# A float32 decoder layer on one core: weights and operands count as ready when their low parts are done, the output projection's late operands are split in its order, and the first two row tiles load first

## The chip, the cores and the metric

The kernel runs on one core of one Trainium2 chip. The time is that of one execution on the device, in microseconds (us); less is better. A core has engines that each run their own instructions in order: TensorE (PE in the rows: matmuls and transposes), VectorE (DVE), ScalarE (ACT), GpSimd (POOL) and SyncE (SP, which here only issues transfers). They wait for each other through semaphores.

## The reference

It is one decoder layer on 512 rows of 1024 float32 values: RMSNorm, an input projection, two token mixers (retention and a gated delta rule) merged by gates, an output projection with a residual, then a gated MLP with a causal convolution.

```python
def reference(x, ...):                      # x (1, 512, 1024) float32
    u = rmsnorm(x, g)
    ret_q, ret_k, ..., gates = split(u @ w_in)
    o_r = retention_chunkwise(...)          # 8 heads
    o_d = gated_delta_chunkwise(...)        # 8 heads, a triangular solve per 128 rows
    h = x + merged(o_r, o_d, gates) @ w_o   # the output projection
    return rmsnorm(h + conv_ffn(rmsnorm(h)))
```

## The kernel before

**Products in parts.** TensorE multiplies float32 values as sums of parts. `split` makes of an operand a high part (a cast, on ScalarE) and a low part (operand minus high part, on VectorE). `weights()` does the same for the weights, in 212 blocks of 128x1024 that are loaded to `wraw`, cast to `whi` and subtracted to `wlo`; four blocks are held at a time. A product is then three matmuls, a **triple**: weight high with operand high, weight high with operand low, weight low with operand high. `take()` gives the next block to a product and holds TensorE's order until the block is in `ready`.

**How the order is made.** The order of instructions on every engine is fixed when the program is built. A planner (`Order`) keeps a clock that TensorE's planned work moves on and for each engine a time at which it is free; tasks (Python generators, started with `spawn`) issue their instructions when the clock passes their time, and `yield 0.3` puts a task off by 0.3 planned us. `hold(cond)` runs tasks until `cond` is met, so that a matmul is placed behind the instructions that make its operands. These times only set the order; on the chip the engines wait for what they need.

**The stages.** The start loads the rows of x in four row tiles of 128 (two halves each), scales them (`norm_in`) and transposes them. The mixing phase follows (projections `pk`, `pq`, `pv`, `pr`, `pz`; two triangular solves in steps `pm`, for which a solved block goes through DRAM, `x_dram`, and comes back as `tt`). Then come four products of 1024x1024 (`py`, whose sums are `res`).

The **output projection** (`po`) is computed as seven products of quarter matrices, p = 0, 5, 2, 3, 4, 1, 6 in that order, with the operands B11, B22, T2, T1, T3, B21, T4. Each has two row tiles (t = 0, 1), four triples each, and two weight blocks; its blocks are #112 to #125. `m_out` takes the transposed merged rows (`mr`, a copy by ScalarE out of `pmt`), forms the operands' sums on VectorE (`mt`: T3 = B22 - B12, T2 = B11 - T3, T1 = B11 - B12, T4 = -T2 - B21) and starts `o_split` for each, whose high and low parts appear as `mB` and `mT`. `o_into` adds a finished product into `h` on VectorE; a row tile of `h` that is complete gets its sum of squares (`junk`, ScalarE), `rs` (VectorE), `rr` (a power, GpSimd), its scaling (`hs`), transposes (`pt`) and the split to `u2hi` (ScalarE) and `u2lo` (VectorE). Row tiles 2 and 3 are complete before 0 and 1; h_20 below is tile 2's first half.

The **FFN** (`pa`, `pb`) starts on row tiles 2 and 3 and takes in tiles 0 and 1 as they come; its weight blocks (`w_up`) begin with #126. The down projection (`pd`) follows.

The names above are those in the rows: an output, an arrow and the inputs. A helper records all of VectorE's and ScalarE's instructions, so that they all have line 200, and all matmuls have line 215, transposes 219.

Of the kernel before, what the change touches and what calls it, by code (L numbers as in the profile page):

```python
# [13 lines left out]
AF = mybir.ActivationFunctionType  # L14
ALU = mybir.AluOpType
# [40 lines left out]
HK = KT // 2  # L56
# [37 lines left out]
BLOCKS = weight_blocks()  # L94
# [3 lines left out]
class Order:  # L98
# [29 lines left out]
    def spawn(self, gen, after=0.0):  # L128
        self.n += 1
        heapq.heappush(self.tasks, ((self.clock if self.now is None else self.now) + after, self.n, gen))  # L130
# [91 lines left out]
def body(nc, tc, ctx, io):  # L222
    sp = nc.sync
    order = Order()
    spawn, poll, hold = order.spawn, order.poll, order.hold
    vec = Engine(order, "vec", nc.vector, vec_cost)
    act = Engine(order, "act", nc.scalar, act_cost)
# [15 lines left out]
    def S(name, dt=F32):  # L243
        return heap.tile([P, T], dt, name=name, tag="s", bufs=HEAP)
# [90 lines left out]
    def weights():  # L335
        i = count["split"]
        if i == len(BLOCKS):
            return
        count["split"] += 1
        while i not in raws:  # L340
            yield 0.3
        raw = raws.pop(i)
        n = raw.shape[1]
        hi = wp.tile([P, n], F32R, name="whi", tag="whi", bufs=WB)
        act.copy(hi, raw)
        yield

        n_ = 0
        while order.free.get("vec", 0.0) > order.now + 0.8 and n_ < 12:
            n_ += 1  # L350
            yield 0.3
        lo = wp.tile([P, n], F32R, name="wlo", tag="wlo", bufs=WB)
        vec.tensor_tensor(lo, raw, hi.bitcast(F32), ALU.subtract)
        ready[i] = (hi, lo)
        yield
        free[0] += 1
        fetch()

# [130 lines left out]
    full = slice(0, T)  # L489
# [34 lines left out]
    def split(dst_hi, dst_lo, src, scale=None):  # L524

        if scale is None:
            act.copy(dst_hi, src)
            yield
            vec.tensor_tensor(dst_lo, src, dst_hi.bitcast(F32), ALU.subtract)
        else:  # L530
            act.activation(dst_hi, src, AF.Identity, scale=scale)
            yield
            vec.scalar_tensor_tensor(dst_lo, src, scale, dst_hi.bitcast(F32), ALU.mult, ALU.subtract)

    def transpose4(src, name):
        pt = PS(name)
# [8 lines left out]
    for t in range(NT):  # L545
        for i in range(2):
            sp.dma_start(x_in[t][i], xv[t, :, ck(i, T)])
        if t == 0:
            sp.dma_start(cst, io["cst"][:, :256])
        if t == 1:  # L550
            sp.dma_start(prm, io["prm"])
            fetch()
    free[0] = 1
# [13 lines left out]
    def norm_in(t):  # L567
        xs = [S(f"xs{t}{i}") for i in range(2)]
        ssq = s4("ssqx", 2)
        for i in range(2):  # L570
            half_ssq(ssq, i, x_in[t][i], xs[i])
        yield
        rr = s4("rr", 1)
        yield from row_scale(ssq, rr)
        yield
        vec.tensor_scalar(xs[0], x_in[t][0], rr, None, ALU.mult)
        if t < 2:
            act.activation(xs[1], x_in[t][1], AF.Identity, scale=rr)
        else:
            pool.tensor_scalar(xs[1], x_in[t][1], rr, None, ALU.mult)  # L580
        xs_all[t] = xs

    for t in range(NT):
        spawn(norm_in(t), (3.4, 4.9, 11.0, 12.6)[t])

    def fetch_more():
        while "G" not in have:
# [665 lines left out]
    def o_get(name, k, t):  # L1253
        return (name, t) in o_opnd and tuple(a[:, ck(k)] for a in o_opnd[name, t])

    def o_split(name, t, src):
        hi, lo = S(f"m{name}", F32R), S(f"m{name}", F32R)
        yield from split(hi, lo, src)
        o_opnd[name, t] = hi, lo

    def m_out(t, i, r):
        yield 0.2
        pt = transpose4(r, "pmt")
        yield
        name, half = f"B{i + 1}{t // 2 + 1}", t % 2
        m = o_raw[name, half] = S(f"mr{t}{i}")
        act.copy(m, pt)
        yield
        if name in ("B11", "B21", "B22"):
            spawn(o_split(name, half, m))  # L1270
        if name == "B12":
            t3 = S("mt3")
            vec.tensor_tensor(t3, o_raw["B22", half], m, ALU.subtract)
            t2 = o_raw["T2", half] = S("mt2")
            vec.scalar_tensor_tensor(t2, t3, -1.0, o_raw["B11", half], ALU.mult, ALU.subtract)
            spawn(o_split("T2", half, t2), 0.2)
            yield 2.5
            t1 = S("mt1")
            vec.tensor_tensor(t1, o_raw["B11", half], m, ALU.subtract)
            spawn(o_split("T1", half, t1), 0.2)  # L1280
            yield 2.5
            spawn(o_split("T3", half, t3), 0.2)
        elif name == "B21":
            yield 1.5
            t4 = S("mt4")
            vec.scalar_tensor_tensor(t4, o_raw["T2", half], -1.0, m, ALU.mult, ALU.subtract)
            spawn(o_split("T4", half, t4), 0.2)
# [59 lines left out]
    h1 = [[None] * 2 for _ in range(NT)]  # L1347
# [13 lines left out]
    def o_into(t, i, ps, op, last=False):  # L1361

        vec.tensor_tensor(h1[t][i], h1[t][i], ps, op)
        yield
        if not last:
            return
        junk = S("junk")
        act.activation(junk, h1[t][i], AF.Square, scale=1.0 / 32.0, accum_out=ssqs[t][:, i:i + 1])
        if i == 0:
            return  # L1370
        yield
        rr = s4("rr", 1)
        yield from row_scale(ssqs[t], rr)
        yield
        for i2 in range(2):
            xs = S("hs")
            vec.tensor_scalar(xs, h1[t][i2], rr, None, ALU.mult)
            spawn(u2_out(t, i2, xs), 0.6 * (i2 + 1))

    u2_ready = set()  # L1380
# [12 lines left out]
    def fourth(t, ps):  # L1393
        yield from o_into(2 + t, 1, ps, ALU.subtract)
        yield from o_into(2 + t, 0, ps, ALU.add, True)

    def bank():
        return [PS("po") for _ in range(2)]

    A = bank()  # L1400
    product(0, o_get, HK, [[(full, A[t], True, o_into(t, 0, A[t], ALU.add))] for t in range(2)])
    E = bank()
    product(5, o_get, HK, [[(full, E[t], True, o_into(2 + t, 0, E[t], ALU.add))] for t in range(2)])
    product(2, o_get, HK, [[(full, A[t], False, o_into(2 + t, 0, A[t], ALU.add))] for t in range(2)])
    F = bank()
    product(3, o_get, HK, [[(full, F[t], True, fourth(t, F[t]))] for t in range(2)])
    product(4, o_get, HK, [[(full, A[t], False, o_into(2 + t, 1, A[t], ALU.subtract, True))] for t in range(2)])
    C = bank()
    product(1, o_get, HK, [[(full, C[t], True, o_into(t, 0, C[t], ALU.add, True))] for t in range(2)])
    product(6, o_get, HK, [[(full, A[t], False, o_into(t, 1, A[t], ALU.subtract, True))] for t in range(2)], tail=2)  # L1410
    u2 = (u2hi, u2lo)
    spawn(presums(presum((DOWN,), 4), (order.clock, order.clock + 200.0, 32)))

# [138 lines left out]
    F = [PS("pd") for _ in range(2)]  # L1552
# [86 lines left out]
```

## Time and profile before

| | |
|---|---|
| median of three runs | 1007.29 us (1005.05 to 1008.56) |
| the profiled execution | 1006.75 us |
| its span, first to last instruction | 1005.0 us |
| mean granted TensorE clock | 0.995 |
| TensorE busy with matmuls | 985.0 us (98%) |
| VectorE busy | 732.5 us (73%) |
| ScalarE busy | 538.8 us (54%) |
| GpSimd busy | 173.1 us (17%) |

The profile is one execution of the program. A row of a timeline gives the start and the duration of an instruction, or of several alike that follow each other (x2), and in brackets the idle time of the engine before it with what ended it. Instructions overlap a little, so the price of one in a full queue is read from the starts of neighbours. The granted clock is a share of TensorE's full 2.4 GHz; the lower of its two levels is 1.2 GHz.

### The profile page before, as it was taken

What the parts mean: (1) busy time and instruction counts of PE and PEld (TensorE: products, weight loads), DVE (VectorE), ACT (ScalarE), POOL (GpSimd) and SP (SyncE); (2) the same over time, 40 slices, a digit from 0 to 9 for tenths busy, and PEclk for the clock granted to TensorE, in tenths of its full rate; (3) what the DMA queues carried; (4) which work ended last, traced back from release to release, by engine and by line L of the source; (5) the groups of instructions that cost most, each with busy time, mean ns of one, the idle gap of its engine ahead of it and who ended that gap; (6) DMA issues with size and microseconds to landing.
All of it is one profiled execution on the core that took longest, in us unless ns stands there. A gap on an engine that the chain in (4) does not pass through costs nothing.

```text
span 1005.0 us, 14343 instructions
## 1 busy us (share of the span) xinstructions
PE 985.0 (98%) x5241; PEld 819.9 (82%) x5241; DVE 732.5 (73%) x1372; ACT 538.8 (54%) x1134; POOL 173.1 (17%) x212
## 2 busy tenths in 40 slices
PE   8999999999999999999999998899999999999997
PEld 7888888788778887888888886798888888888886
DVE  5867698557687796666799888865656667678785
ACT  5599222267945422576786645654443433346663
POOL 3031322223343120131000000121112221000001
PEclk9999999999999999999999998999999999999999
DMA  7243669877796693469965844556669999346663
GB/s 266 81 145 111 190 194 242 235 156 194 197 206 183 181 235 119 127 174 292 253 222 189 272 151 142 173 195 221 224 192 202 229 197 211 105 118 207 188 195 120
DMA packets 82230, 189.29 MB, mean 188 GB/s; under 512 B 22704, under 2 KB 31216, under 8 KB 82160
## 3 DMA queue, kind: packets, MB, share of 16 engines
q1 hardware_dynamic: 54640, 123.36, 37.7%
q0 software_dynamic: 27520, 65.02, 29.3%
q8 instruction: 41, 0.67, 0.3%
q14 instruction: 29, 0.24, 0.1%
HBM read 185.17 MB, written 68.19 MB: 252 GB/s over the span
## 4 chain that ended last, share of the span: by engine, by line
PE 89%; DVE 4%; ACT 2%; issue 2%; DMA 1%; POOL 1%; SPq 0%; POOLq 0%; DVEq 0%
PE py L215 14%; PE pa L215 12%; PE pb L215 12%; PE pd L215 10%; PE pz L215 9%; PE pr L215 9%; PE pk L215 4%; PE pq L215 4%; PE pv L215 4%; PE po L215 3%; PE psc L215 3%; PE pm L215 1%; PE pro L215 1%; DVE wlo L200 1%; DMA gb<-g_dram 1%
## 5 line engine op out<-in xcount | busy, mean ns | idle before, releaser
L200 ACT CAST whi<-wraw 128x1024 fp32r<-128x1024 f32 x212 | 219.4, 1035 | 155.7 <-PE pr L215 55.3
L200 DVE TENSOR_TENSOR wlo<-wraw,whi 128x1024 fp32r<-128x1024 f32 x212 | 254.0, 1201 | 64.6 <-ACT whi L200 64.3
L200 POOL TENSOR_SCALAR tock<-tick 128x1 f32<-128x1 f32 x72 | 34.8, 484 | 395.3 <-ACT tick L200 395.3
L200 DVE SCALAR_TENSOR_TENSOR acc<-pb,prm,acc 128x511 f32<-128x511 f32 (+1 forms) x44 | 33.0, 749 | 57.0 <-ACT acc L200 56.2
L215 PE MATMUL pa<-u2lo,whi 128*128 128x512 f32 (+1 forms) x192 | 71.6, 373 | 2.3 <-DVE u2lo L200 2.3
L215 PE MATMUL pa<-u2hi,whi 128*128 128x512 f32 (+1 forms) x192 | 71.5, 373 | 1.4 <-ACT u2hi L200 1.4
L215 PE MATMUL pa<-u2hi,wlo 128*128 128x512 f32 (+1 forms) x192 | 71.3, 371 | 0.0
L215 PE MATMUL pb<-u2lo,whi 128*128 128x512 f32 (+1 forms) x184 | 69.9, 380 | 0.0
L215 PE MATMUL pb<-u2hi,whi 128*128 128x512 f32 (+1 forms) x184 | 69.9, 380 | 0.0
L215 PE MATMUL pb<-u2hi,wlo 128*128 128x512 f32 (+1 forms) x184 | 69.9, 380 | 0.0
L215 PE MATMUL py<-whi,oh 128*128 128x512 f32 x160 | 62.6, 392 | 0.0
L215 PE MATMUL py<-wlo,oh 128*128 128x512 f32 x160 | 62.3, 389 | 0.0
L215 PE MATMUL py<-whi,ol 128*128 128x512 f32 x160 | 62.3, 389 | 0.0
L215 PE MATMUL pd<-whi,T 128*128 128x512 f32 (+1 forms) x198 | 55.4, 366 | 0.0
L215 PE MATMUL pz<-uhi,whi 128*128 128x512 f32 x128 | 52.5, 410 | 0.0
L215 PE MATMUL pr<-whi,uhi 128*128 128x512 f32 x128 | 50.9, 398 | 0.0
L215 PE MATMUL pz<-uhi,wlo 128*128 128x512 f32 x128 | 50.0, 391 | 0.0
L215 PE MATMUL pr<-whi,ulo 128*128 128x512 f32 x128 | 49.9, 390 | 0.0
L215 PE MATMUL pz<-ulo,whi 128*128 128x512 f32 x128 | 49.9, 390 | 0.0
L215 PE MATMUL pr<-wlo,uhi 128*128 128x512 f32 x128 | 49.8, 389 | 0.0
L200 DVE SCALAR_TENSOR_TENSOR acc<-pa,prm,acc 128x511 f32<-128x511 f32 (+1 forms) x44 | 32.9, 749 | 19.0 <-ACT acc L200 18.3
L215 PEld LDWEIGHTS pa<-u2lo,whi 128*128 128x128 f32 x192 | 36.1, 188 | 9.0 <-DVE u2lo L200 2.7
(318 smaller groups left out, 2459.5 us busy)
## 6 DMA issues: line engine op xcount, KB each, us to landing
wraw<-w SPq DMA_DIRECT2D x100, 512.0 KB, 4.5
s<-wm POOLq DMA_DIRECT2D x30, 1024.0 KB, 6.8
wraw<-s SPq DMA_DIRECT2D x60, 512.0 KB, 3.7
s<-wd POOLq DMA_DIRECT2D x24, 704.0 KB, 5.2
wraw<-wm SPq DMA_DIRECT2D x30, 512.0 KB, 4.4
s<-s POOLq DMA_DIRECT2D x10, 1024.0 KB, 12.9
wraw<-wd SPq DMA_DIRECT2D x15, 512.0 KB, 3.6
s<-s POOLq DMA_DIRECT2D x8, 704.0 KB, 8.9
```

Source lines behind the costliest of these rows:

```text
L200: return f(out, *args, **kw)
L215: self.engine.matmul(out, lhsT, rhs, start=start, stop=stop, **kw)
```

## The change

It has six parts. In `weights()`, the loop that held back a low part while VectorE's planned queue was long is gone, except for `w_up`, and a block counts as ready only when its low part has been issued and done in the plan. `split` ends with a `yield`, so that an operand counts as ready after its low part too. At the start, the first two row tiles of x load ahead of the constants, the parameters and the first weight block. In the output projection, operands T3, B21 and T4 are split only once the product 2, 3 or 4 places along the order has begun (`o_now` counts the products), and T4's sum waits in the same way. Product 4 (T3) finishes row tile 0 ahead of row tile 1 (`tail=2`). The scaling of the first half of each complete row tile goes to ScalarE.

```diff
@@ weights()
-        n_ = 0
-        while order.free.get("vec", 0.0) > order.now + 0.8 and n_ < 12:
-            n_ += 1
-            yield 0.3
+        if BLOCKS[i][1] == "w_up":
+            end = order.clock + 6.0
+            while order.free.get("vec", 0.0) > order.now + 0.8 and order.now < end:
+                yield 0.3
         lo = wp.tile([P, n], F32R, name="wlo", tag="wlo", bufs=WB)
         vec.tensor_tensor(lo, raw, hi.bitcast(F32), ALU.subtract)
+        yield
         ready[i] = (hi, lo)
-        yield
@@ split()
             vec.scalar_tensor_tensor(dst_lo, src, scale, dst_hi.bitcast(F32), ALU.mult, ALU.subtract)
+        yield
@@ loads at the start
-        if t == 0:
+        if t == 1:
             sp.dma_start(cst, io["cst"][:, :256])
-        if t == 1:
             sp.dma_start(prm, io["prm"])
             fetch()
@@
-        spawn(norm_in(t), (3.4, 4.9, 11.0, 12.6)[t])
+        spawn(norm_in(t), (3.4, 4.4, 11.0, 12.6)[t])
@@ output projection
+    o_now = [-1]
+    o_since = {"T3": 2, "B21": 3, "T4": 4}
+
     def o_split(name, t, src):
+        while o_now[0] < o_since.get(name, -1):
+            yield 0.5
         hi, lo = S(f"m{name}", F32R), S(f"m{name}", F32R)
@@ m_out()
-        if name in ("B11", "B21", "B22"):
+        if name != "B12":
             spawn(o_split(name, half, m))
@@
-            yield 2.5
+            yield 0.5
             t1 = S("mt1")
             vec.tensor_tensor(t1, o_raw["B11", half], m, ALU.subtract)
             spawn(o_split("T1", half, t1), 0.2)
-            yield 2.5
             spawn(o_split("T3", half, t3), 0.2)
         elif name == "B21":
-            yield 1.5
+            while o_now[0] < 3:
+                yield 0.5
             t4 = S("mt4")
@@ o_into()
-            vec.tensor_scalar(xs, h1[t][i2], rr, None, ALU.mult)
+            if i2:
+                vec.tensor_scalar(xs, h1[t][i2], rr, None, ALU.mult)
+            else:
+                act.activation(xs, h1[t][i2], AF.Identity, scale=rr)
@@
+    def o_product(p, accs, tail=0):
+        o_now[0] += 1
+        product(p, o_get, HK, accs, tail)
...
-    product(4, o_get, HK, [[(full, A[t], False, o_into(2 + t, 1, A[t], ALU.subtract, True))] for t in range(2)])
+    o_product(4, [[(full, A[t], False, o_into(2 + t, 1, A[t], ALU.subtract, True))] for t in range(2)], tail=2)
```

The first place is VectorE's order ahead of T2. These are the rows before, from the low part of block #115 to that of #116, the first block of T2 (`mB` low parts of B11, B21 or B22, `mt` and `mT` of the T's):

```order
L200 TENSOR_TENSOR wlo<-wraw,whi 128x1024
L200 SCALAR_TENSOR_TENSOR mt_6339<-mt_6288,mr_6304 128x512
L200 TENSOR_TENSOR mB_6324<-mr_6304,mB_6323 128x512
L200 TENSOR_TENSOR h_00_5873<-h_00_5873,po 128x512
L200 TENSOR_TENSOR mT_6342<-mt_6339,mT_6341 128x512
L200 TENSOR_TENSOR mB_6349<-mr_6334,mB_6348 128x512
L200 TENSOR_TENSOR h_10_5877<-h_10_5877,po 128x512
L200 SCALAR_TENSOR_TENSOR mt_6365<-mt_6308,mr_6334 128x512
L200 TENSOR_TENSOR mt_6373<-mr_6020,mr_6271 128x512
L200 TENSOR_TENSOR mT_6371<-mt_6365,mT_6370 128x512
L200 TENSOR_TENSOR wlo<-wraw,whi 128x1024
```

And these are the rows of the change, again from #115 to #116 and on to #117:

```order
L200 TENSOR_TENSOR wlo<-wraw,whi 128x1024
L200 TENSOR_TENSOR mt_6290<-mr_6168,mr_6273 128x512
L200 SCALAR_TENSOR_TENSOR mt_6292<-mt_6290,mr_6022 128x512
L200 TENSOR_TENSOR mt_6299<-mr_6193,mr_6285 128x512
L200 SCALAR_TENSOR_TENSOR mt_6301<-mt_6299,mr_6050 128x512
L200 TENSOR_TENSOR mT_6297<-mt_6292,mT_6296 128x512
L200 TENSOR_TENSOR mT_6307<-mt_6301,mT_6306 128x512
L200 TENSOR_TENSOR wlo<-wraw,whi 128x1024
L200 TENSOR_TENSOR h_00_5873<-h_00_5873,po 128x512
L200 TENSOR_TENSOR h_10_5877<-h_10_5877,po 128x512
L200 TENSOR_TENSOR mt_6355<-mr_6022,mr_6273 128x512
L200 TENSOR_TENSOR wlo<-wraw,whi 128x1024
```

The sums and splits of B21 and T4, a sum of T1 and the additions into `h` no longer stand between the two low parts; the six sums and splits of T3 and T2, which stood between #114 and #115, now stand behind #115. From #113 to #116 there were 24 instructions of 128x512 besides the two `wlo` between, and there are 15.

The second place is VectorE's order at the end of T4 and the start of the FFN. Before (the `rs` are those of row tiles 2 and 3; the `wlo` ahead of h_00 is #126, the later one #127):

```order
L200 SCALAR_TENSOR_TENSOR rs<-ssq_6259 128x1
L200 TENSOR_TENSOR wlo<-wraw,whi 128x1024
L200 TENSOR_TENSOR h_00_5873<-h_00_5873,po 128x512
L200 SCALAR_TENSOR_TENSOR rs<-ssq_6260 128x1
L200 TENSOR_TENSOR h_10_5877<-h_10_5877,po 128x512
L200 TENSOR_TENSOR h_01_5875<-h_01_5875,po 128x512
L200 TENSOR_SCALAR hs<-h_20_5881,rr 128x512
L200 TENSOR_SCALAR hs<-h_21_5883,rr 128x512
L200 TENSOR_SCALAR hs<-h_30_5885,rr 128x512
L200 TENSOR_SCALAR hs<-h_31_5887,rr 128x512
L200 TENSOR_TENSOR wlo<-wraw,whi 128x1024
```

And in the change, from #125 on:

```order
L200 TENSOR_TENSOR wlo<-wraw,whi 128x1024
L200 SCALAR_TENSOR_TENSOR rs<-ssq_6261 128x1
L200 TENSOR_TENSOR h_00_5873<-h_00_5873,po 128x512
L200 TENSOR_TENSOR h_10_5877<-h_10_5877,po 128x512
L200 SCALAR_TENSOR_TENSOR rs<-ssq_6262 128x1
L200 TENSOR_TENSOR wlo<-wraw,whi 128x1024
L200 TENSOR_SCALAR hs<-h_21_5883,rr 128x512
L200 TENSOR_TENSOR wlo<-wraw,whi 128x1024
L200 TENSOR_TENSOR h_01_5875<-h_01_5875,po 128x512
L200 TENSOR_SCALAR hs<-h_31_5887,rr 128x512
```

Both `wlo`, #126 and #127, now stand ahead of h_31's scaling, and h_20 and h_30 are scaled on ScalarE: there the order is the square of h_00, the scaling of h_20, the square of h_10, the scaling of h_30, the sixteen `u2hi`. Further on, VectorE has h_11 among the sixteen `u2lo`, then `rs` of row tile 0, `wlo` #128 and #129, `rs` of row tile 1 and h_01's scaling; before, `rs` of tile 0 stood behind four of them, its two scalings behind thirteen, and #128 after those.

On TensorE the transposes of row tiles 2 and 3 stood two and one triples ahead of T4's end. Now the four of h_20 come at the end of T4's row tile 0, with four triples of tile 1 left, and the twelve of h_21, h_30 and h_31 one triple later; those of row tile 0 come after 11 triples of the FFN, those of tile 1 seven triples on. In the mixing phase the first `pm` step of a solve stands 15 `pr` matmuls earlier, and nine `pr` matmuls lie between it and the second step, where there were 15.

## Rows read from the trace of the kernel before

**Rows 1.** The engines' waits, TensorE: us in all, times, longest.

```profile
PE po L215 <- DVE wlo L200: 3.7, 1, 3.7
PE pt L219 <- DVE xs L200: 2.5, 2, 1.7
```

**Rows 2.** Windows: busy us (and instructions) of each engine, granted clock, DMA share, GB/s.

```profile
17.00:585.00 568.00, 566.72 (x3261) 469.79 (x3259) 426.10 (x881) 322.04 (x747) 121.67 (x133) 1.00 0.69 191
...
615.00:621.00 6.00, 6.00 (x17) 4.71 (x17) 5.32 (x8) 3.13 (x4) 0.00 (x0) 0.60 0.54 162
...
646.00:660.00 14.00, 9.63 (x75) 9.03 (x76) 10.19 (x29) 7.71 (x28) 4.04 (x6) 1.00 0.57 182
```

**Rows 3.** TensorE's timeline, T2's start to T4: start, duration.

```profile
610.35 0.61 PE L215 MATMUL po<-whi,mT 128*128 128x512 f32 x2
...
619.90 0.39 PE L215 MATMUL po<-wlo,mT 128*128 128x512 f32 x1
...
642.37 0.39 PE L215 MATMUL po<-wlo,mT 128*128 128x512 f32 x1
```

**Rows 4.** VectorE's timeline ahead of T2, from block #113 to #116.

```profile
593.07 1.22 DVE L200 TENSOR_TENSOR wlo<-wraw,whi 128x1024 fp32r<-128x1024 f32 x1
...
603.35 0.69 DVE L200 TENSOR_TENSOR mT<-mt,mT 128x512 fp32r<-128x512 f32 x1 [0.69 <-ACT mT L200]
...
609.01 0.68 DVE L200 TENSOR_TENSOR h<-h,po 128x512 f32<-128x512 f32 x1
609.61 0.68 DVE L200 TENSOR_TENSOR mT<-mt,mT 128x512 fp32r<-128x512 f32 x1
...
613.38 1.22 DVE L200 TENSOR_TENSOR wlo<-wraw,whi 128x1024 fp32r<-128x1024 f32 x1
614.52 0.69 DVE L200 TENSOR_TENSOR mT<-mt,mT 128x512 fp32r<-128x512 f32 x1
```

**Rows 5.** ScalarE's timeline: the high part of block #116.

```profile
605.93 1.05 ACT L200 CAST whi<-wraw 128x1024 fp32r<-128x1024 f32 x1
```

**Rows 6.** TensorE's timeline at the start of the FFN.

```profile
647.31 0.38 PE L215 MATMUL pa<-u2hi,whi 128*128 128x256 f32 x1 [1.37 <-ACT u2hi L200]
...
648.82 0.28 PE L215 MATMUL pa<-u2hi,whi 128*128 128x256 f32 x1
...
649.52 0.28 PE L215 MATMUL pa<-u2hi,whi 128*128 128x256 f32 x1
...
658.55 1.09 PE L219 MATMUL pt<-cst,hs 128*128 128x128 f32 x8 [0.71 <-DVE hs L200]
659.40 0.37 PE L215 MATMUL pa<-u2hi,whi 128*128 128x256 f32 x1
```

**Rows 7.** VectorE's timeline at the start of the FFN.

```profile
638.24 1.23 DVE L200 TENSOR_TENSOR wlo<-wraw,whi 128x1024 fp32r<-128x1024 f32 x1
...
642.04 1.67 DVE L200 TENSOR_SCALAR hs<-h,rr 128x512 f32<-128x512 f32 x4
...
647.04 2.42 DVE L200 SCALAR_TENSOR_TENSOR u2lo<-pt,prm,u2hi 128x128 fp32r<-128x128 f32 x9 [0.30 <-ACT u2hi L200]
```

**Rows 8.** GpSimd's timeline: `rr` of row tiles 2 and 3.

```profile
638.38 1.53 POOL L200 TENSOR_TENSOR rr<-rs,mhalf 128x1 f32<-128x1 f32 x1 [145.42 <-DVE rs L200]
640.22 0.56 POOL L200 TENSOR_TENSOR rr<-rs,mhalf 128x1 f32<-128x1 f32 x1 [0.31 <-DVE rs L200]
```

**Rows 9.** ScalarE's timeline at the start: a scaling of x.

```profile
8.21 0.72 ACT L200 ACTIVATE xs<-x,rr 128x512 f32<-128x512 f32 x1
```

**Rows 10.** Instructions on tile tt, 170 to 192 us: durations in ns, starts; landing.

```profile
L215 PE MATMUL pm<-tt,A x16: 191/191/212, 188.2 to 188.4; 32*32 32x32 f32 x16
L886 SPq DMA_DIRECT2D tt<-x_dram x4: 325/488/489, 179.1 to 180.6; - x4
...
DMA to landing us min/median/max: 3.8/4.1/4.3
```

**Rows 11.** VectorE's timeline in the first solve.

```profile
190.07 0.60 DVE L200 TENSOR_SCALAR m<-pm 32x128 f32<-32x128 f32 x2
```

More of the change, by code (lines that the diff above doesn't have):

```diff
@@ L1398, in bank @@
         return [PS("po") for _ in range(2)]
+    def o_product(p, accs, tail=0):
+        o_now[0] += 1
+        product(p, o_get, HK, accs, tail)
     A = bank()
-    product(0, o_get, HK, [[(full, A[t], True, o_into(t, 0, A[t], ALU.add))] for t in range(2)])
+    o_product(0, [[(full, A[t], True, o_into(t, 0, A[t], ALU.add))] for t in range(2)])
     E = bank()
-    product(5, o_get, HK, [[(full, E[t], True, o_into(2 + t, 0, E[t], ALU.add))] for t in range(2)])
-    product(2, o_get, HK, [[(full, A[t], False, o_into(2 + t, 0, A[t], ALU.add))] for t in range(2)])
+    o_product(5, [[(full, E[t], True, o_into(2 + t, 0, E[t], ALU.add))] for t in range(2)])
+    o_product(2, [[(full, A[t], False, o_into(2 + t, 0, A[t], ALU.add))] for t in range(2)])
     F = bank()
-    product(3, o_get, HK, [[(full, F[t], True, fourth(t, F[t]))] for t in range(2)])
-    product(4, o_get, HK, [[(full, A[t], False, o_into(2 + t, 1, A[t], ALU.subtract, True))] for t in range(2)])
+    o_product(3, [[(full, F[t], True, fourth(t, F[t]))] for t in range(2)])
+    o_product(4, [[(full, A[t], False, o_into(2 + t, 1, A[t], ALU.subtract, True))] for t in range(2)], tail=2)
     C = bank()
-    product(1, o_get, HK, [[(full, C[t], True, o_into(t, 0, C[t], ALU.add, True))] for t in range(2)])
-    product(6, o_get, HK, [[(full, A[t], False, o_into(t, 1, A[t], ALU.subtract, True))] for t in range(2)], tail=2)
+    o_product(1, [[(full, C[t], True, o_into(t, 0, C[t], ALU.add, True))] for t in range(2)])
+    o_product(6, [[(full, A[t], False, o_into(t, 1, A[t], ALU.subtract, True))] for t in range(2)], tail=2)
     u2 = (u2hi, u2lo)
```

## The prediction

> **What bounds the kernel now.** I read the engines' waits first. TensorE is the engine that ends last, and its longest wait by far is one of 3.7 us in the output projection: a `po` matmul held by VectorE's `wlo`; the two at the program's start sum to 2.5 [rows 1]. The windows by stage then show where else it loses time. From 17 to 585 us it is busy 566.72 of 568 us, so what the change reorders there can cost but hardly gain. The two stretches with losses are the one at this wait, after which, from 615 to 621, the granted clock is 0.60, so mostly the lower level (1.2 GHz) and not 2.4, and 646 to 660, where the FFN starts and TensorE is busy 9.63 of 14 us at clock 1.00 [rows 2].
>
> TensorE's timeline gives the size of the first loss. T2's first `whi` matmuls start at 610.35, and the fifth `wlo` matmul, the fifteenth of the product, at 619.90. From there to 642.37 are 33 triples, 99 matmuls, in 22.47 us: 0.227 us each [rows 3]. At that pitch 14 steps take 3.2 us; they took 9.55. So 6.4 us are lost: 3.7 waiting and 2.7 at the lower clock after it.
>
> Why that `wlo` (block #116, the first of T2's two) is late stands in VectorE's timeline. Block #113 starts at 593.07, #116 at 613.38, done when the next starts, 614.52. Between lie 24 512-wide instructions, each 0.60 us after the one before (609.01, 609.61), two `wlo` at 1.14 (613.38 to 614.52) and waits such as the 0.69 on ScalarE [rows 4]. #116's high part was being made at 605.93 [rows 5], 7.4 us before VectorE came to the low part. So neither the transfer nor the cast is the cause: VectorE's order is.
>
> The second loss: from T2's start at 610.35 to `pa` after the last transposed tile (659.40) are 49.05 us. The work in it: 40 triples of 0.68 (27.2), 18 FFN triples of 0.35 (648.82 to 649.52 are two), and four groups of eight transposes of 0.85 (658.55 to 659.40) [rows 3, 6]: 27.2 + 6.3 + 3.4 = 36.9. So 12.1 us are lost, 6.4 at T2 and 5.7 at the FFN's start, of which 1.37 and 0.71 stand in the rows shown [rows 6].
>
> **Low parts at T2.** The order shows 15 instead of 24 512-wide instructions between #113 and #116: nine that stood there, the operands of B21 and T4, one step of T1's and two additions into `h`, now come later. If #113 starts where it did, #116 ends at 593.07 + 1.14 + 15 x 0.60 + 3 x 1.14 = 606.6; for waits on ScalarE such as the 0.69 and pairs that depend on each other I add 1.4: 608.0. The late bound keeps all of the old waits: 614.52 - 9 x 0.60 = 609.1. TensorE needs it two matmuls into T2, 610.35 + 0.45 = 610.8. Both ends come before, so T2's 6.4 us go.
>
> **What is late next.** The nine instructions are moved, not removed. I walk VectorE's new order from 608.0 with those prices. T1's operands and block #118 are done by 613.9, T1 starts at 615.8. T3's by 618.6, against 621.25. In T3 the tile t=0 now runs to its end before t=1, so its second block (#121) is needed after two triples instead of four, at 623.05; with 1.2 us of waits on ScalarE, VectorE finishes it at 623.4: a wait of 0.35. T4 then starts at 632.5; its blocks #124 and #125 are done at 632.1 and 633.9, needed at 632.5 and 633.9: no wait, and no reserve.
>
> At T4 the walk goes on against TensorE. T4's t=0 half ends at 610.35 + 36 x 0.68 + 0.35 = 635.2. There now come four transposes of h_20, which ScalarE scales. No 512-wide scaling of `h` by ScalarE is in the trace; the nearest row is the same operation on `x`, 0.72 us [rows 9] (VectorE's is 0.40, four in 1.67 [rows 7], the lower end; I take 0.72, the same engine and form). ScalarE has it behind the square of h_00, done about 635.3: the scaled tile is there at 636.0, a wait of 0.8. After one triple come h_21 (VectorE, done 636.95, in time), h_30 and h_31. Ahead of h_31 VectorE now has `wlo` #127 and h_01: done 639.1, TensorE there at 638.0, a wait of 1.1. Three triples later, at 641.6, the FFN starts; VectorE's sixteen `u2lo` take 0.27 each (nine in 2.42 [rows 7]), with h_11 between them, and run until 644.0: a wait of about 0.3. Eleven triples on, at 645.75, TensorE wants tile t=0. Its `rs` stands behind all `u2lo` (644.0), and two `wlo` (#128, #129) stand right behind it, before `hs_01`. GpSimd's `rr` took 1.53 us when a `wlo` ran beside it (638.24), 0.56 otherwise [rows 7, 8]. Held through both `wlo`, it ends near 646.95, and with ScalarE's 0.72 and passing on the tile is there at 648.0, a wait of 2.25. Not held, VectorE's own place for `hs_01` decides, 647.1, a wait of 1.35. I take 2.25, since the rows with a `wlo` beside them are the ones that this place is like.
>
> The Trainium skill's GPSIMD Engine Reference, section 1 "Specifications", says that GpSimd shares its SBUF interfaces with VectorE and contends with VectorE instructions that have two SBUF inputs. A `wlo` has two, so this trace agrees (1.53 against 0.56), and the rule speaks against a place where two of them follow `rs`; without it the sum below would be 0.9 us lower, 998.6.
>
> The last tile follows seven triples later without a wait: 648.0 + 0.85 + 2.45 + 0.85 = 652.15, where before it was 659.40. **New waits: 0.35 + 0.8 + 1.1 + 0.3 + 2.25 = 4.8 us in place of 12.1.** None is as long as the 3.7 that was followed by the lower clock; after the wait of 1.37 the window's clock is 1.00 [rows 2, 6], so I add nothing for the clock. Bounds: with none of the four waits at T4 and the FFN's start the gain is 11.7; with the old 5.7 there it is 6.0.
>
> **The start.** x's second row tile now loads ahead of `prm`, but `ba_lo`, which needs `prm`, stands in VectorE's order ahead of both scalings, so the transposes wait as now. Bounds: all 2.5 us of waits gone [rows 1], or the first weight's cast 0.72 later behind one more scaling [rows 9]. I take 0.
>
> **The mixing phase.** Without the delay loop, low parts move up in VectorE's order, and the triangular solves' TensorE steps with them: the first `pm` step stands 15 `pr` matmuls (3.4 us) earlier, and the second comes 9 matmuls after it instead of 15. 9 x 0.227 + 0.4 = 2.4 us, where VectorE needs its two `m` (0.60 [rows 11]) and some 0.5 to pass on. The transferred `tt` landed 4.3 us or less after an issue at 180.6, by 184.9, and was wanted at 188.2 [rows 10]: 3.3 us of slack against the 3.4. The solve's VectorE steps also begin earlier in the order, which I don't count. I take 0; bounds 0 and some 4 us (0.5 at each of eight heads).
>
> The removed holding-back itself is hidden: those `wlo` run anyway, under TensorE's matmuls. If that cover went, each early one ahead of a needed instruction would cost 1.14.
>
> **Sum.** 1006.75 (the profiled execution; span 1005.0 and 1.75 around it) - 12.1 + 4.8 = 999.5 us. It is 0.5 below the median of the three runs shown; a shift of that size either way is inside the range. About 0.3%, 3 us, is what a measurement of this kernel can tell from no change.
>
> **Rivals.**
> - *The FFN's start loses its waits too* (0.15): For it: ScalarE takes every second scaling from VectorE, and four of the five waits are short. Against: t=0's `rs` now stands in front of two `wlo`. With most of the 4.8 gone: about 996.
> - *VectorE becomes the bound of the whole projection* (0.12). For it: no reserve at #121, #124 and #125. Against: it was idle at times before. If it is 1.5 us later at T3 and again at T4, 3 us of waits and 2.7 us of the lower clock: 999.5 + 5.7 = 1005, no change.
> - *It does not do what it says at T2* (0.08): something else, such as the block's transfer, holds the low part. Rows 5 speaks against it. Then only 5.7 - 4.45 is won: 1005.5.
> - *Slower: the solve's transfer* (0.05). If VectorE, with `wlo`s moved up ahead of the solve's steps, issues it later, TensorE waits at its first `pm` in both solves. With the lower clock after each, 3.4 us late costs 2 x (3.4 + 2.7) = 12.2: 1011.7. It decides from 10.3 us in all (7.3 won and 3 more), that is from about 2.5 us late in both.
>
> **How the numbers follow.** The forecast has 0.60, between 997 and 1002.5. Range 995.5 to 1005.2: it takes in the first two rivals and the start's and mixing's bounds, and leaves out the other two and tails, some 0.2. Faster: 0.60 + 0.15 + 0.05 from the milder part of the second and third, 0.80; same 0.14; slower 0.06 (the last rival and mishaps of the first phase).
>
> **What would show it.** Right: no `po` wait on `wlo` at T2's start and clock 1.00 from 611 to 621; T2's start to the last transposed tile near 42 us; the largest waits left at the FFN's start, `pt` on `hs` of t=0 about 2 us, beside an `rr` of well over 1 us. Wrong: a clock below 1.00 anywhere from T2 to the FFN; `pm` matmuls in the list of waits; `pa` waits as before.

## The result and the profile after

The change is faster by 0.7%: 999.98 us median of four runs (999.57 to 1000.93) against 1007.61 of four before, a ratio of 0.993, 95% interval 0.991 to 0.9949. The profiled execution took 999.83 us, span 998.1. The forecast was 999.5, between 995.5 and 1005.2.

TensorE's waits after the change, to be read against [rows 1] (us in all, times, longest):

```profile
PE pt L219 <- DVE xs L200: 3.7, 3, 2.5
PE pt L219 <- ACT hs L200: 2.1, 2, 1.6
...
PE pt L219 <- DVE hs L200: 0.7, 1, 0.7
```

The wait of 3.7 us at T2 and all `pa` waits (2.3 on `u2lo` and 1.4 on `u2hi` before) are gone. What is left from T2 on are 0.2 for a low part and, for scaled tiles of `h`, 2.1 on ScalarE, which is new, and 0.7 on VectorE, which was 0.7 before. The start's waits for scaled tiles of x are 3.7 where they were 2.5. No `pm` is in the list: the triangular solves do not wait.

The windows of the same stretches (columns as in [rows 2]):

```profile
17.00:585.00 568.00, 565.75 (x3251) 468.70 (x3249) 425.21 (x881) 318.80 (x742) 115.19 (x134) 1.00 0.68 190
...
615.00:621.00 6.00, 6.00 (x28) 4.95 (x28) 6.00 (x8) 5.67 (x8) 0.00 (x0) 1.00 0.42 139
...
639.00:653.00 14.00, 11.76 (x89) 10.85 (x88) 11.02 (x33) 10.98 (x35) 4.30 (x6) 1.00 0.66 223
```

After T2's start the clock is 1.00 where it was 0.60, and TensorE does 28 matmuls in these 6 us instead of 17. At the FFN's start it is busy 11.76 of 14 us (9.63 before). The mixing phase stays full.

T2's place in TensorE's timeline, with T3's second block and the transposes of `h`:

```profile
611.21 0.62 PE L215 MATMUL po<-whi,mT 128*128 128x512 f32 x2
611.66 0.39 PE L215 MATMUL po<-wlo,mT 128*128 128x512 f32 x1
...
624.30 0.50 PE L215 MATMUL po<-wlo,mT 128*128 128x512 f32 x1 [0.23 <-DVE wlo L200]
...
636.87 0.66 PE L219 MATMUL pt<-cst,hs 128*128 128x128 f32 x4 [0.49 <-ACT hs L200]
...
639.83 0.66 PE L219 MATMUL pt<-cst,hs 128*128 128x128 f32 x4 [0.68 <-DVE hs L200]
...
648.16 1.09 PE L219 MATMUL pt<-cst,hs 128*128 128x128 f32 x8 [1.56 <-ACT hs L200]
...
652.54 0.36 PE L215 MATMUL pa<-u2hi,whi 128*128 128x256 f32 x1
```

T2's first low part follows 0.45 us after T2's start, with no wait. From T2's start to `pa` after the last transposed tile are 652.54 - 611.21 = 41.33 us, where there were 49.05 [rows 3, 6].

VectorE at the same places: the low part of #116 and what follows it, then the end of the sixteen `u2lo`:

```profile
607.81 1.22 DVE L200 TENSOR_TENSOR wlo<-wraw,whi 128x1024 fp32r<-128x1024 f32 x1 [0.26 <-ACT whi L200]
608.96 1.28 DVE L200 TENSOR_TENSOR h<-h,po 128x512 f32<-128x512 f32 x2
...
644.49 0.15 DVE L200 SCALAR_TENSOR_TENSOR rs<-ssq 128x1 f32<-128x1 f32 x1
644.55 2.35 DVE L200 TENSOR_TENSOR wlo<-wraw,whi 128x1024 fp32r<-128x1024 f32 x2
```

Block #116 is done at 608.96, 2.25 us ahead of T2's start; before it was done 4.2 us behind it (614.52 against 610.35 [rows 3, 4]). GpSimd after that `rs` (`tock` waits for `tick`, a copy that ScalarE makes: so the program paces the transfers that GpSimd issues):

```profile
644.38 0.22 POOL L200 TENSOR_SCALAR tock<-tick 128x1 f32<-128x1 f32 x1 [6.69 <-ACT tick L200]
644.89 0.83 POOL L200 DMA_DIRECT2D s<-wd  x1 [0.29 <-issue]
645.75 1.60 POOL L200 TENSOR_TENSOR rr<-rs,mhalf 128x1 f32<-128x1 f32 x1
```

`rr` of row tile 0 begins 1.1 us after `rs` is done, behind a transfer that GpSimd issues. It then takes 1.60 us. Of the two `wlo` only the second runs beside it: that one starts 1.14 after 644.55, at 645.69, and ends at 646.90, and `rr` ends at 647.35, 0.45 later.

### The profile page after: what moved, and what is told of

It reads as the page before. It is cut to its first block, busy times and chain, and to the rows that moved or that the text cites. A ratio compares the mean times of both kernels' runs of the same rounds, so it can differ in the third digit from the quotient of the medians.

```text
span 998.1 us, 14344 instructions
## 1 busy us (share of the span) xinstructions
PE 982.0 (98%) x5241; PEld 817.9 (82%) x5241; DVE 730.8 (73%) x1368; ACT 538.3 (54%) x1134; POOL 167.2 (17%) x212
## 4 chain that ended last, share of the span: by engine, by line
PE 93%; DVE 3%; DMA 1%; issue 1%; POOL 1%; ACT 1%; SPq 0%; POOLq 0%; DVEq 0%; ACTq 0%
PE py L215 15%; PE pb L215 12%; PE pa L215 12%; PE pd L215 10%; PE pz L215 9%; PE pr L215 9%; PE pk L215 4%; PE pv L215 4%; PE pq L215 4%; PE psc L215 3%; PE pm L215 2%; PE po L215 1%; PE pro L215 1%; DVE wlo L200 1%; PE pkk L215 1%
## 5 line engine op out<-in xcount | busy, mean ns | idle before, releaser
L200 POOL TENSOR_SCALAR tock<-tick 128x1 f32<-128x1 f32 x72 | 32.8, 455 | 408.6 <-ACT tick L200 408.5
L200 ACT ACTIVATE acc<-pb,prm 128x512 f32<-128x512 f32 x22 | 17.2, 781 | 48.5 <-PE pb L215 48.5
```

What stands on the lines that cost most here:

```text
L200: return f(out, *args, **kw)
```

## The experiments

The order of all engines is made by one planner, so that most edits change it in several places. The table therefore splits each profiled execution at T2's first matmul: its time in TensorE's timeline, and the span minus that time. Start and mixing lie ahead of it, the rest of the output projection and the FFN behind. Ratios are to the kernel before. The two last columns are of one execution each: that of f1 took 1003.39 us, 1.7 above its median, and that of e4 1001.08, 1.5 below. T2's start also varies between executions by some 2 us: f1's order is that of before on all engines up to 597 us, and its T2 starts 2.1 us later.

| kernel | median us | ratio, 95% interval | T2's start | from there to the end |
|---|---|---|---|---|
| before | 1007.61 | | 610.35 | 394.6 |
| the change | 999.98 | 0.993 (0.991 to 0.9949) | 611.21 | 386.9 |
| e1_loop_only | 1010.5 | 1.0027 (1.0017 to 1.0037) | 613.79 | 395.0 |
| e2_osplit_only | 1001.55 | 0.9936 (0.9924 to 0.9949) | 611.90 | 387.9 |
| e3_no_load | 1002.76 | 0.9949 (0.9937 to 0.9962) | 614.24 | 387.0 |
| e4_no_hs | 1002.62 | 0.9951 (0.9938 to 0.9965) | 611.21 | 388.2 |
| f1_wo_loop | 1001.68 | 0.9942 (0.993 to 0.9955) | 612.47 | 389.0 |
| f2_fill | 1006.59 | 0.9988 (0.9979 to 0.9996) | 611.07 | 393.2 |
| f3_late_pt | 998.61 | 0.9909 (0.9895 to 0.9923) | 611.23 | 385.4 |
| f4_rr_free | 1000.19 | 0.9925 (0.9911 to 0.9938) | 611.53 | 386.9 |
| g1_weights | 1001.15 | 0.9942 (0.993 to 0.9954) | 613.16 | 386.2 |
| g2_no_ready | 1003.57 | 0.9963 (0.9951 to 0.9976) | 611.73 | 390.0 |
| g3_no_tail | 1003.25 | 0.9958 (0.9945 to 0.9972) | 611.96 | 390.0 |
| g4_best | 1003.25 | 0.996 (0.9947 to 0.9972) | 611.56 | 390.3 |

**e1_loop_only.** The kernel before, with the loop in `weights()` as in the change.

```diff
-        n_ = 0
-        while order.free.get("vec", 0.0) > order.now + 0.8 and n_ < 12:
-            n_ += 1
-            yield 0.3
+        if BLOCKS[i][1] == "w_up":
+            end = order.clock + 6.0
+            while order.free.get("vec", 0.0) > order.now + 0.8 and order.now < end:
+                yield 0.3
```

> The kernel before with one part of the change alone: the loop that held low parts back is gone (kept for w_up). Its order has 15 instead of 24 512-wide VectorE instructions between blocks #113 and #116, as the whole change. Theory (VectorE's order, which this loop set, is the cause of T2's wait): no po wait on wlo at T2, 6.4 us back. At the FFN's start the walk gives a first wait of about 2 us on u2lo (the low part of #127 and h_11 stand among them) and no wait for tiles 0 and 1: 36.9 + 2 = 39 us from T2's start to the last transposed tile, so about 997 to 998.5 us, and the output projection's other edits would be worth nothing or less. Rival (the operands' later splitting is what frees VectorE at T2): T2's wait stays at 3 us or more and the time within 1 us of before, 1006 to 1008.

It was slower than before, 1010.5. The theory held at T2 and fell everywhere else. TensorE's waits in the timeline from T1 on:

```profile
620.58 0.50 PE L215 MATMUL po<-whi,mT 128*128 128x512 f32 x1 [0.96 <-DVE mT L200]
627.75 0.50 PE L215 MATMUL po<-whi,mT 128*128 128x512 f32 x1 [1.26 <-DVE mT L200]
648.57 0.39 PE L215 MATMUL pa<-u2lo,whi 128*128 128x256 f32 x1 [1.87 <-DVE u2lo L200]
660.50 0.58 PE L215 MATMUL pa<-u2hi,wlo 128*128 128x256 f32 x1 [3.45 <-DVE wlo L200]
```

Nothing waits for a low part at T2. But a wait of the same kind and size, 3.45 us for a `wlo`, now stands in the FFN, and the operands' parts (`mT`) are late at two places: the same VectorE work in another order. The granted clock fell behind two of these waits, to 0.68 from 650 to 655 and 0.66 from 660 to 665. Ahead of T2 it also lost 3.4 us (613.79 against 610.35), 1.5 of it in the start, whose order is that of before, and 1.6 in a new wait of `psc`.

**g1_weights.** e1 with readiness as in the change: the low part done before a block counts, and `split`'s `yield`.

```diff
         vec.tensor_tensor(lo, raw, hi.bitcast(F32), ALU.subtract)
-        ready[i] = (hi, lo)
         yield
+        ready[i] = (hi, lo)
...
+        yield
```

> The kernel before with the weights' part whole: the loop gone (kept for w_up), a block and an operand ready only after the low part. Beside the run with the loop alone this adds only the readiness. Theory (the loop alone lost because the order let TensorE reach a w_up block whose low part came late, a pa wait of 3.4 us with the lower clock behind it; readiness in the plan prevents it): no pa wait on wlo, some 2.2 us of po waits on mT and about 2 at T4 and the FFN's start: 1000 to 1001. Rival (readiness changes nothing, the w_up block is late again): 1005 or more.

1001.15: as the theory said, to 0.2 us. The 3.45 is gone, the two `mT` waits stay (2.2 in all), and from T2's start to the end it takes 386.2 us, no more than the whole change. So the weights' part alone brings the whole gain of that stretch; what it lacks lies ahead of T2 (613.16). That the median met the theory is in part luck: the waits of about 2 us at T4 and the FFN's start are not in its list, and the time ahead of T2 was not in the sum.

**g2_no_ready.** The change with `ready[i]` set ahead of the `yield` as before, `split` kept.

```diff
-        yield
         ready[i] = (hi, lo)
+        yield
         free[0] += 1
```

> The changed kernel, with a weight block counted as ready as soon as its low part is placed (as before) instead of one step later. Theory (with the operands in their order, the plan no longer runs ahead of VectorE, so this part is worth little here): the order differs at the FFN's start alone, 999.5 to 1000.5. Rival (it is what keeps w_up's low parts ahead of TensorE): a pa wait on wlo of about 3 us, 1003 or more.

1003.57, slower than the theory allowed, but without the rival's wait on `wlo`. TensorE's waits at the FFN's start, and below them the window behind:

```profile
641.94 0.38 PE L215 MATMUL pa<-u2hi,whi 128*128 128x256 f32 x1 [0.43 <-ACT u2hi L200]
643.35 0.39 PE L215 MATMUL pa<-u2lo,whi 128*128 128x256 f32 x1 [1.03 <-DVE u2lo L200]
647.67 1.97 PE L219 MATMUL pt<-cst,hs 128*128 128x128 f32 x8 [2.57 <-ACT hs L200]
```

```profile
645.00:650.00 5.00, 2.43 (x12) 2.33 (x12) 2.93 (x9) 3.18 (x9) 1.71 (x3) 0.50 0.73 246
```

The low part of #127 came later in VectorE's order, and the first two waits are for the parts of `u2` around it. The third is not VectorE's: `rs` of tile 0 was done at 643.03, earlier than in the change, but `rr` began at 646.27, behind a `tock` (644.88) and a transfer (645.41) in GpSimd's queue. The three waits, none as long as 3.7, were followed by the lower clock (0.50, 1.2 GHz). Neither theory had that.

**e2_osplit_only.** The kernel before with the operands split in the products' order (`o_now`, `o_since` and the yields of `m_out`, as in the change's diff).

```diff
     def o_split(name, t, src):
+        while o_now[0] < o_since.get(name, -1):
+            yield 0.5
```

> The kernel before with only the operands of the output projection split in its order (o_now, the shorter yields, T4's sum later). 20 instead of 24 instructions stand ahead of #116, so it ends near 614.5 - 2.4 = 612.1 and T2 waits 1.3 us instead of 3.7. Theory (the lower clock after T2's wait is a matter of that one long wait): clock 1.00 after it; with some 2.5 us of waits at T4 and the FFN's start, 999 us. Rival (any wait there brings the lower clock for the same 2.7 us): 1001.7 us. If the order of the operands alone does nothing: 1007.

T2's wait was 1.30 us, as worked out from 20 instructions, and the clock stayed:

```profile
613.82 0.50 PE L215 MATMUL po<-wlo,mT 128*128 128x512 f32 x1 [1.30 <-DVE wlo L200]
```

```profile
612.00:618.00 6.00, 4.70 (x21) 3.54 (x20) 6.00 (x9) 4.24 (x6) 0.00 (x0) 1.00 0.46 138
```

TensorE's order is that of before up to 640 us; VectorE's and ScalarE's differ from 606 us on. From T2's start it won 6.7 us. The median of 1001.55 is that of the rival, but its reason is not: T2 started 1.55 us later than before, 1.52 of it from the program's start, whose order was that of before (the transposes `pbt`, which end the start, stand at 31.64 instead of 30.12).

**f1_wo_loop.** The kernel before, the loop skipped for ten blocks.

```diff
-        while order.free.get("vec", 0.0) > order.now + 0.8 and n_ < 12:
+        while not 112 <= i < 122 and order.free.get("vec", 0.0) > order.now + 0.8 and n_ < 12:
```

> The kernel before, with the loop that holds low parts back skipped for ten blocks of the output projection alone (#112 to #121); up to T2 the order of all engines is that of before. 14 instead of 24 VectorE instructions stand ahead of #116. Theory (that loop made T2's wait; but without the operands' later splitting the freed place is paid by operands that come late): no wait for the low part at T2, clock 1.00 there, 6.4 us back, and some 2.2 us of new waits of po on mT at T1 and T3, as in the run with the loop gone everywhere: 1003 us. Rivals: all of it is kept, 1001; all of it is given back, 1007.

1001.68: the median is 1.3 below the theory's sum and nearer to the rival that keeps all (1001), but the waits are the theory's: none for a low part in `po`, three on `mT`, 2.3 in all, and clock 1.00 through the stage. 5.6 us were won behind T2's start. The order is that of before up to 597 us only; from there on, beside the low parts, some `pmt` transposes and `mr` copies moved too.

**f2_fill.** The kernel before with extra matmuls in T2's wait.

```diff
                 pe.matmul(ps, xlo, whi[:, kk, c], start=False, stop=False, skip_group_check=True)
+                if name == "T2" and opnd is o_get and k == 0 and t == 0:
+                    fill = PS("fill")
+                    for _ in range(16):
+                        nc.tensor.matmul(fill, xhi, whi[:, kk, c], start=True, stop=True)
```

> The kernel before, with 16 extra matmuls (T2's own first operands, into a bank of their own that nobody reads) between T2's second and third matmul, in the planner's eyes without time: TensorE works through the 3.7 us in which it waited. 16 x 0.227 = 3.6 us, so the third matmul comes no later than before. Theory (2.7 of the 6.4 us are the lower clock that follows the idle time): clock 1.00 after it, 2.7 us faster than before, 1005.0. Rival (the slow matmuls after the wait have another cause): as before, 1007.7.

TensorE's timeline of T2:

```profile
611.07 0.61 PE L215 MATMUL po<-whi,mT 128*128 128x512 f32 x2
611.52 3.79 PE L457 MATMUL fill<-whi,mT 128*128 128x512 f32 x16
615.40 0.50 PE L215 MATMUL po<-wlo,mT 128*128 128x512 f32 x1
...
619.12 0.50 PE L215 MATMUL po<-wlo,mT 128*128 128x512 f32 x1 [0.70 <-DVE wlo L200]
```

Before, the first low matmul was this one:

```profile
614.65 0.80 PE L215 MATMUL po<-wlo,mT 128*128 128x512 f32 x1 [3.69 <-DVE wlo L200]
```

The clock stayed at 1.00 (windows 608 to 615 and 615 to 621). From the first low matmul to the fifth are 619.12 - 615.40 = 3.72 us, and 3.02 without the wait; before they were 619.90 - 614.65 = 5.25. So 2.2 of the 2.7 us were the lower clock behind the idle time. But the time fell by only 0.9: TensorE, now quicker, met the next low part, #117, 0.70 us too early, and #116 itself is as late as ever. 0.9 is nearer to the rival's 0 than to the theory's 2.7; the clock rows, not the time, speak for the theory.

**e3_no_load.** The change with the loads at the start as before.

```diff
-        if t == 1:
+        if t == 0:
             sp.dma_start(cst, io["cst"][:, :256])
+        if t == 1:
             sp.dma_start(prm, io["prm"])
...
-        spawn(norm_in(t), (3.4, 4.4, 11.0, 12.6)[t])
+        spawn(norm_in(t), (3.4, 4.9, 11.0, 12.6)[t])
```

> The changed kernel with the loads at the start in the order of before. Theory (the load order is worth 0, as predicted; T2's start stands 0.86 us later in the changed kernel's profile because of the mixing phase's new order): the same time as the change within 0.5 us, 999.5 to 1000.5. Rival (the load order costs those 0.86 us): 999.1.

1002.76: theory and rival both fell. With the other edits in place the new load order is worth 2.8 us by the medians and 3.0 by T2's start, and little of that lies at the start. `pbt` stands at 31.28 here, 30.89 in the change and 30.12 before; in the three runs e2, f1 and f2, whose start is that of before to the instruction, at 31.0 to 31.6. So the start itself varies by more than the load order moves it. The loss is in the mixing phase, in new waits, of which the list has these (us, times, longest):

```profile
PE proT L219 <- DVE ro L200: 1.2, 1, 1.2
...
PE pvt L219 <- ACT o L200: 0.7, 1, 0.7
```

and 0.6 for `pot`. The shifted times at the start gave the planner another order: TensorE's differs from that of the change from 65 us on, and these waits stand at 245, 277 and 451 us. g1, which has the old loads too, reached T2 2 us later than the change, with the same kind of waits (`pvt` 1.0, `pot` 0.6).

**e4_no_hs.** The change with both scalings of a row tile on VectorE.

```diff
-            if i2:
-                vec.tensor_scalar(xs, h1[t][i2], rr, None, ALU.mult)
-            else:
-                act.activation(xs, h1[t][i2], AF.Identity, scale=rr)
+            vec.tensor_scalar(xs, h1[t][i2], rr, None, ALU.mult)
```

> The changed kernel with both halves of each row tile of h scaled on VectorE, as before. Theory (at T4 and the FFN's start VectorE is the later engine, but ScalarE has its share behind squares and casts): waits of 1.7 at h_20, 0.2 at h_31, about 1.2 on u2lo and some 1.5 for tile 0, 4.5 in all, as in the changed kernel: the same within 0.7 us. Rival (the scaling on ScalarE is what relieves VectorE there): 1.6 us or more slower, 1001.6 and up.

1002.62, 2.6 us slower by the medians. The profiled execution, with 1001.08 the fastest of its five, shows 1.3 of it, all behind T2's start (388.2 against 386.9). The rival was nearer. Two waits are left, both for tiles that VectorE scales: 1.32 for h_20, which ends at 637.72, and this one:

```profile
647.27 0.66 PE L219 MATMUL pt<-cst,hs 128*128 128x128 f32 x4 [2.54 <-DVE hs L200]
```

Behind the second stands GpSimd: `rs` was done at 643.55, `rr` began at 646.11 behind a transfer (645.25), and VectorE was idle for 1.00 us before it could scale tile 0. So only the first speaks for the rival's reason.

**g3_no_tail.** The change without `tail=2` in T3.

```diff
-    o_product(4, [[(full, A[t], False, o_into(2 + t, 1, A[t], ALU.subtract, True))] for t in range(2)], tail=2)
+    o_product(4, [[(full, A[t], False, o_into(2 + t, 1, A[t], ALU.subtract, True))] for t in range(2)])
```

> The changed kernel without tail=2 in T3. T3's second block is then needed two triples later, so the wait of 0.23 us there goes; the transposes of tiles 2 and 3 come two and one triples before T4's end and those of tile 0 right at the FFN's start. Theory (what is won is given back, the waits at T4 and the FFN's start are VectorE's): the same as the change within 1 us, 999 to 1001. Rival (finishing tile 0 of T3 first is what brings the row tiles early): 1002 or more.

1003.25: the rival. The wait of 0.23 in T3 is gone, and one of 4.75 us for tile 0's transposes right at the FFN's start takes its place, with a clock of 0.72 in the window 645 to 650. There `rr` was done early, at 641.24; the scaling on ScalarE stood behind sixteen `u2hi` and two casts of 128x1024, until 645.86.

**f3_late_pt.** The change with tile 0's transposes later.

```diff
-            spawn(u2_out(t, i2, xs), 0.6 * (i2 + 1))
+            spawn(u2_out(t, i2, xs), 0.6 * (i2 + 1) + (2.4 if t == 0 else 0.0))
```

> The changed kernel, with the transposes of row tile 0 placed six triples later in TensorE's order at the FFN's start; nothing else moves but the second scalings of tile 1, one place. Theory (the wait of 1.56 us for tile 0 is only where the transposes stand): 1.5 us faster than the change, 998.5. Rival (the wait goes on to tile 1's transposes or to the pa matmuls behind them): the same as the change, 1000.

998.61, as the theory had it: behind T2's start 1.5 us less than the change, its wait of 1.56. This is the fastest kernel of the study.

**f4_rr_free.** The change with #128's and #129's low parts behind tile 0's scaling (`scaled` is a list to which `o_into` adds the tile once it is scaled).

```diff
+            end = order.clock + 12.0
+            while i in (128, 129) and not scaled and order.now < end:
+                yield 0.1
         lo = wp.tile([P, n], F32R, name="wlo", tag="wlo", bufs=WB)
```

> The changed kernel, with the low parts of #128 and #129 behind the scaling of row tile 0 in VectorE's order instead of between rs and that scaling. Theory (a wlo beside it holds GpSimd's rr): rr takes about 0.6 instead of 1.60 us, the wait for tile 0 shrinks from 1.56 to about 0.5: 999.0. Rival (rr is long for another reason, such as the transfer issued ahead of it on GpSimd): rr stays at 1.6 and the time at 1000.

GpSimd's row for both `rr`, and TensorE's waits:

```profile
646.09 1.15 POOL L200 TENSOR_TENSOR rr<-rs,mhalf 128x1 f32<-128x1 f32 x2
```

```profile
647.49 1.53 PE L219 MATMUL pt<-cst,hs 128*128 128x128 f32 x12 [0.54 <-ACT hs L200]
649.93 0.66 PE L219 MATMUL pt<-cst,hs 128*128 128x128 f32 x4 [0.91 <-DVE hs L200]
```

`rr` takes 0.58 each instead of 1.60 and the wait for tile 0 fell from 1.56 to 0.54: the theory's mechanism is shown. `rr` still began 1.1 us after `rs`, behind the transfer. The time is the rival's, 1000.19, since the planner also drew tile 1's transposes seven triples forward, where a new wait of 0.91 stands.

**g4_best.** The change with three row tiles' transposes later.

```diff
-            spawn(u2_out(t, i2, xs), 0.6 * (i2 + 1))
+            spawn(u2_out(t, i2, xs), 0.6 * (i2 + 1) + (2.4, 0.0, 0.7, 0.7)[t])
```

> The changed kernel with the transposes later in TensorE's order: row tile 0 by 2.4 planned us, tiles 2 and 3 by 0.7 (one triple). Theory (what is left of the waits at T4 and the FFN's start is where the transposes stand): beside the run with tile 0 alone later, the waits of 0.45 for h_20 and 0.67 for h_31 go too: 997.5. Rival (u2's parts come as much later, and the FFN's start waits for them instead): 998.6 as that run.

1003.25, worse than both. TensorE's waits, the window behind, and VectorE's scaling of tile 0:

```profile
641.80 0.39 PE L215 MATMUL pa<-u2hi,whi 128*128 128x256 f32 x1 [0.44 <-ACT u2hi L200]
643.56 0.38 PE L215 MATMUL pa<-u2lo,whi 128*128 128x256 f32 x1 [1.37 <-DVE u2lo L200]
647.73 0.58 PE L215 MATMUL pa<-u2lo,whi 128*128 128x256 f32 x1 [2.40 <-DVE u2lo L200]
```

```profile
645.00:650.00 5.00, 2.60 (x13) 2.31 (x12) 3.13 (x8) 1.94 (x5) 3.19 (x6) 0.50 0.69 239
```

```profile
646.93 0.49 DVE L200 TENSOR_SCALAR hs<-h,rr 128x512 f32<-128x512 f32 x1 [1.52 <-POOL rr L200]
```

The waits for the scaled tiles are gone and their successors are longer. Tiles 2 and 3 came one triple later, and the planner let a `wlo` in ahead of their `u2lo`; among the `u2lo`, ahead of the last four, it put another `wlo` and the scaling of tile 0. VectorE stood idle 1.52 us for that scaling's `rr`: `rs` was done at 641.25, but `rr` began at 646.30, behind a transfer (645.45) on GpSimd. The FFN waited 1.37 and 2.40 us for `u2lo`, with the lower clock behind.

## Why the prediction was right

**Low parts at T2.** Right in cause and size. Predicted: #116 done at 608.0, T2 at 610.35, so 2.35 us ahead; measured 2.25 ahead. That TensorE's 6.4 us there hung on VectorE's order is shown by e2, where four VectorE instructions fewer made the 3.7 into 1.30 with TensorE's own order as before, and by f1, where ten fewer took the wait away. f2 shows the two halves of the 6.4: filling the idle time took the lower clock away, 2.2 us of 2.7. Which edit clears VectorE the prediction left open: the loop does, 24 to 15 instructions (e1, g1); the operands' later splitting alone goes only to 20. The edits do not add up: of the 7.7 us that the change wins behind T2's start, the operands' splitting alone wins 6.7 (e2) and the weights' part alone 8.4 (g1).

**What is late next.** Predicted waits 0.35, 0.8, 1.1, 0.3 and 2.25, 4.8 in all; measured 0.23, 0.49, 0.68, none and 1.56, 3.0 in all. Four of the five places and their order were right, each wait was sized too high, and the stretch came out at 41.33 us instead of 41.8. That closeness is partly luck: with 36.9 us of work the waits of 3.0 would give 39.9. A row's idle time leaves out part of a delay (636.87 stands 0.65 after its place by the pitch, with 0.49 idle); by the starts the four delays are 0.40, 0.65, 0.92 and 1.72, 3.7 in all, and the work around them took 37.6, not 36.9. The two errors, 1.1 too much and 0.7 too little, cancel for the greater part. How little slack the order has there, e4, g2, g3 and g4 show: small edits of it lose 1.3 to 3.4 us behind T2's start, and f3 wins 1.5.

**`rr` held by `wlo`.** That a `wlo` lengthens `rr` is shown (0.58 in f4 against 1.60). The Trainium skill's GPSIMD Engine Reference, section 1 "Specifications", says that GpSimd shares its SBUF interfaces with VectorE, with contention from VectorE instructions that have two SBUF inputs. A `wlo` has two, and this trace agrees (1.60 beside a `wlo`, 0.58 without).

But "held through both" is not what happened. In e2 and f1 `rr` began beside the first of two `wlo`, took 1.51 and 1.49 us and ended 0.43 and 0.45 after that first one, while the second ran. In the change `rr` met the second `wlo` alone, because it began 1.1 us late behind a transfer that GpSimd issues (0.83 us). So the forecast's end, near 646.95 with T2 at 610.35, was nearly met (647.35 with T2 at 611.21), but by another path: a transfer and one `wlo`, not two `wlo`. In e2 and f1 a small `rs` stands between the two, in the change nothing does; whether `rr` would have come between them there is not shown. The prediction took `rr` alone out of GpSimd's queue. The same transfer stands ahead of `rr` in the kernel before, where `rs` of tile 0 was done at 646.74 (TensorE had no wait from it there):

```profile
649.41 0.83 POOL L200 DMA_DIRECT2D s<-wd  x1
650.27 0.59 POOL L200 TENSOR_TENSOR rr<-rs,mhalf 128x1 f32<-128x1 f32 x1
```

With this transfer and its `tock` ahead of it, `rr` of tile 0 began 2.56, 3.24 and 5.05 us after its `rs` in e4, g2 and g4, and the longest wait of each hung on it. No run moves the transfer, so what that would win is not shown. The sentence that freeing `rr` would be worth 0.9 us did not come true: f4 gave it all back at tile 1.

**The start and the mixing phase, taken as 0.** The sum was right: T2 starts at 611.21 instead of 610.35, 0.8 of it in the start, which varies by as much between runs. The solves did not wait, as worked out. But that the rest of the mixing phase cost nothing was luck: the prediction walked the solves alone, and e3 shows that with the old load order the same edits lose 2.8 us, in waits there at `proT`, `pvt` and `pot`. The bounds (0 to 4) held that much.

**No charge for the clock.** Right here, clock 1.00 from 597 to 653. The reason given, that no wait was as long as 3.7, would not have carried: in g2 and g4 waits of 1.0 and 2.6, or 1.4 and 2.4, were followed by 1.2 GHz, and in e1 a single one of 1.87.

**The rivals.** That VectorE becomes the bound of the whole projection did not happen in the change; in e1 it did, at the FFN. That the change does nothing at T2 is excluded by #116's row. The waits at the FFN's start went in part. The solve's transfer did not make it slower: no `pm` waits.

What stays open: why the start took 30.1 us in one execution and up to 31.6 in others with the same instructions, which of the changed orders in the mixing phase makes e3's waits, and what a later transfer on GpSimd at the FFN's start would win.

## What to carry to other kernels

Where one engine makes parts for several consumers, a wait is a matter of its queue: count the instructions ahead of the late one, multiply by the pitch of neighbours (from one's start to the next one's), and walk on to the next consumer, since removed instructions are mostly moved ones. Walk every queue that the late item passes, with all that stands in it: here a transfer on GpSimd, the least busy engine, was left out. Such a walk with measured pitches came within 0.5 us over 41, partly since its errors cancelled; single edits of the order won or lost 1 to 3 us in ways that no busy share shows. And when a plan decides the order, try an edit together with what it does elsewhere: the loop alone made this kernel slower, with the readiness rule it gave the whole gain of its stage.

## What the runs showed of the hardware

TensorE's clock fell behind waits that are each shorter than the one of 3.7 us: it was 0.50 from 645 to 650 behind waits of 0.44, 1.37 and 2.40 that ended at 641.80, 643.56 and 647.73 (g4), and the same behind 0.43, 1.03 and 2.57 (g2). In e1 one wait of 1.87, the only one in its rows from 640 to 655, that ended at 648.57 was followed by 0.68 from 650 to 655. But waits of 1.32 and 2.54 that ended at 637.72 and 647.27 (e4) left it at 1.00 in every window of 5 us from 605 to 670, and so did waits of 1.37, 0.78 and 1.57 that ended at 647.31, 648.47 and 652.09 in the kernel before, from 645 to 660. So neither the longest wait nor their sum tells here whether the clock falls.

GpSimd's power of 128 values took 0.58 us alone and 1.38 to 1.60 with a 128x1024 subtraction beside it on VectorE; where it began beside the subtraction it ended 0.41 to 0.45 us after it (before, the change, e1, e2, e4, f1). A transfer that the same queue issues takes 0.83 us and holds the power behind it for that long or, where the transfer itself is late, longer.
